# Where a two-layer diffusion block computes its second layer's modulation

## The chip, the cores and the metric

The kernel runs on one core of a Trainium2 chip. The metric is the device time of one execution in microseconds (us). A core has TensorE (PE; its weight loads run beside it as PEld), VectorE (DVE), ScalarE (ACT), GpSimd (POOL) and SyncE (SP, whose queue issues most transfers). Each engine takes its own instructions in order, and waits by semaphores for the others. Sixteen DMA engines move data between HBM and the on-chip memory.

## The reference

The block has two layers over 512 latent and 256 context tokens of width 1024. Layer 0 mixes by a bidirectional RWKV-7 recurrence and S5 channel groups, layer 1 by latent attention; each layer ends in a mixture of 16 experts. What the change touches:

```python
for layer in range(DEPTH):                       # DEPTH = 2
    m_l = split(silu(c) @ mod_w[layer] + mod_b[layer], 6)      # mod_w: 2 x 1024 x 6144 f32
    m_c = split(silu(c_ctx) @ mod_w[layer] + mod_b[layer], 6)
    a = modulate(rmsnorm(h, norm1_g[layer]), m[0], m[1])
    o = rwkv_s5_mixer(a, ...) if layer == 0 else mla_mixer(a, ...)
    h = h + m[2] * o
    f = modulate(rmsnorm(h, norm2_g[layer]), m[3], m[4])
    h = h + m[5] * moe_ffn(f, ...)
# in the recurrence: k_dir = k * (1 + (a - 1) * k_a); each token: S = S*w - sa*(a*kk) + v*k_dir; y = S @ r
# behind it, by token: (groupnorm(y) * ln_w + ln_b + bonus) * g
```

## The kernel before

The tokens are six tiles of 128. The program is written with a tile framework whose scheduler orders each engine's instructions by a model of their times; what is written early is not always placed early.

**Recurrence.** Steps s = 0 to 5 go over the tiles, forward and backward at once. For each step rwkv_stage_a (L544 and around it) makes decayed factors PQ and KB: VectorE writes the sums `wseg` (L518, L519) from the tile `ev`, scans them into E (L528), and the key factor passes through ACT (L544, scale and bias of `ta`), POOL (L546, times k) and DVE (L547, times E), using `ev` again as scratch. rwkv_stage_b then builds the matrices of a chunk: G from PE products (L572, L575); a 16 x 16 block of it goes through memory into A; X, a triangular inverse, is made on DVE by 15 pairs of L596 and L598; X is written out (L601) and comes back as D (L604). PE, ACT and DVE pass it on: pd0 (L612), Ta (L613), pd1 (L616), W (L617), pd2 (L620), G += (L624, eight DVE instructions), then pt20 to pt22 (L632, L637, L642) with ACT copies Tb between. rwkv_steps runs two half steps per tile: pU, VU, pZ (L697 to L704) and Z += (L706). The chain from G through X, D, G to Z is serial; S5 products (L1108, L1112), the outputs and the modulation are placed around it.

**Outputs.** rwkv_out(t) takes a tile's sums, normalizes them, gates them (gd, L746 to L750; pgate on PE) and stores them (18 larger DVE instructions for two tiles, L755 to L776). It is called at s = 3 for tiles 0 and 1, at s = 4 for 4 and 3, at s = 5 for 5 and 2. concat transposes them (ptcat, L1957) for the output projection.

**Modulation.** mod_part(l, q) makes a third of a layer's six vectors: 16 tiles `mw` of 512 KB from SP's queue (L162) through three buffers, eight matmul records each (L164, psmod), then bias and gain on DVE (L167, L169). The table MODN says behind which step the second layer's parts are written:

```python
MODN = {3: (0,), 4: (1,), 5: (2,)}
...
            if s in MODN:
                for q in MODN[s]:
                    self.mod_part(1, q, mp, ms, MODT)
```

Part 0 is used by the attention's input, parts 1 and 2 only behind the attention.

**Behind the experts** of layer 0 the kernel gathers each tile's expert outputs (POOL, cy), adds them to h (normed), transposes (ntt, L301), projects down (mla_down: pmi, L191 to L193, pmt), makes values (pv), and starts attention with pqp.

Of the kernel before, what the change touches and what calls it, by code (L numbers as in the profile page):

```python
# [16 lines left out]
F32 = mybir.dt.float32  # L17
# [3 lines left out]
AF = mybir.ActivationFunctionType  # L21
OP = mybir.AluOpType
# [13 lines left out]
ZT = ((0, 1, 2, 3, 4, 5), (1, 0, 5, 4, 3, 2))  # L36
# [8 lines left out]
MS14 = (4, 0, 5, 1, 6, 2, 7, 3, 12, 8, 9, 10, 11, 13)  # L45
MODT = "lo"
S5LATE = -800
MODN = {3: (0,), 4: (1,), 5: (2,)}


def dap(ap, offset, dims):
# [36 lines left out]
class Block:  # L88
# [35 lines left out]
    def cond(self, tp):  # L124
        nc, i = self.nc, self.i
        cr = tp.tile([16, 128], F32, name="cr")
        nc.sync.dma_start(cr[0:8, :], i["c"].rearrange("b (k p) -> (b k) p", p=128))
        nc.sync.dma_start(cr[8:16, :], i["c_ctx"].rearrange("(k p) -> k p", p=128))
        cs = tp.tile([16, 128], F32, name="csil")
        nc.scalar.activation(cs, cr, AF.Tanh, scale=0.5)  # L130
        nc.vector.tensor_scalar(cs, cs, 0.5, 0.5, op0=OP.mult, op1=OP.add)
        nc.vector.tensor_tensor(cs, cs, cr, OP.mult)
        pt = self.psum("tp", "pt_c", 2)
        nc.tensor.transpose(pt[:, :16], cs, self.ident[:16, :16])
        self.cst = self.c0.tile([128, 8, 32], F32, name="cst")
        nc.gpsimd.memset(self.cst, 0.0)
        nc.vector.tensor_copy(self.cst[:, :, 0:2], pt[:, :16].rearrange("p (v k) -> p k v", v=2))

    def mod_part(self, l, q, wpool, spool, tag="mod"):

        nc, i = self.nc, self.i
        if l not in self.mods:
# [13 lines left out]
            nc.vector.tensor_scalar(mb[r0:r0 + 64, :], mb[r0:r0 + 64, :], 1.0, None, op0=OP.add)  # L156
        ps = self.psum(tag, f"psmod{l}{q}", 1)
        for k in range(8):
            for h in range(2):
                wt = wpool.tile([128, 4, 256], F32, name=f"mw{l}{q}{k}{h}", tag="mw")  # L160
                w = i["mod_w"][l, k * 128:(k + 1) * 128, q * 2048:q * 2048 + 2048].rearrange("p (j c) -> p j c", j=4)
                last = nc.sync.dma_start(wt, w[:, :, 256 * h:256 * h + 256])  # L162
                for j in range(4):
                    nc.tensor.matmul(ps[32 * j:32 * j + 32, 256 * h:256 * h + 256], self.cst[:, k, :], wt[:, j],  # L164
                                     start=(k == 0 and h == 0), stop=(k == 7), skip_group_check=True)
        mo = mb
        nc.vector.tensor_tensor(mo, ps, mb, OP.add)  # L167
# [309 lines left out]
    def rwkv_stage_a(self, s, sp, wp, tag=("gr",), bufs=2):  # L477

        nc = self.nc
        st = {}  # L480
        for z in range(2):
# [6 lines left out]
            ta = wp.tile([128, 4, 128], F32, name=f"ta{z}{s}", tag="ta", bufs=2)  # L488
# [15 lines left out]
            ev = wp.tile([128, 4, 128], F32, name=f"ev{z}{s}", tag="ev", bufs=2)  # L504
# [16 lines left out]
            for k in range(2):  # L521
                E = wp.tile([128, 8, 65], F32, name=f"E{k}{z}{s}", tag=f"E{k}", bufs=1)
                f = E.rearrange("p a b -> p (a b)")
# [15 lines left out]
            r, k, kk = rk[:, 0:4], rk[:, 4:8], rk[:, 8:12]  # L539
            nc.vector.tensor_tensor(put(PQ[:, :, 64:192]), spl(kk), ei, OP.mult)  # L540
            nc.vector.tensor_tensor(ends(PQ), spl(r), e1, OP.mult)
            t1 = ev
            for m in range(4):
                nc.scalar.activation(t1[:, m, :], ta[:, m, :], AF.Identity, scale=self.hka[:, 0, m:m + 1],  # L544
                                     bias=self.hka[:, 1, m:m + 1])
            nc.gpsimd.tensor_tensor(t1, t1, k, OP.mult)  # L546
            nc.vector.tensor_tensor(ends(KB), spl(t1), e3, OP.mult)  # L547
            nc.scalar.activation(ta, ta, AF.Copy, scale=-0.5, bias=-0.5)
            nc.gpsimd.tensor_tensor(ta, ta, kk, OP.mult)
            nc.vector.tensor_tensor(put(KB[:, :, 64:192]), spl(ta), e3, OP.mult)  # L550
# [880 lines left out]
        nc.vector.tensor_tensor(hh, hh, ps[:, 256:], OP.mult)  # L1431
        return hh

    def row_psum(self, rows, name):

        out = [self.psum("cb", f"{name}{hf}", 2) for hf in range(2)]
        for j in range(8):
            self.nc.tensor.matmul(out[j // 4][:, j % 4 * 128:j % 4 * 128 + 128], self.ident[0:8, j:j + 1].to_broadcast([8, 128]),
                                  rows, start=True, stop=True, skip_group_check=True)
        return out  # L1440
# [174 lines left out]
    def mla_values(self, t):  # L1615

        nc = self.nc
        ts = slice(t * 128, t * 128 + 128)
        for hh in range(2):
            hs = slice(hh * 8, hh * 8 + 8)  # L1620
            ps = self.psum("ca", f"pv{t}{hh}", 2)
            self.mm3(ps, (self.kvT[0][:, ts], self.kvT[1][:, ts]), [x[:, hs, :].rearrange("p h c -> p (h c)") for x in self.kw],
                     True, True)
            dst, src = self.vv[:, t, hs], ps.rearrange("p (h c) -> p h c", h=8)
            if hh:
                nc.vector.tensor_copy(dst, src)
            else:
                nc.scalar.activation(dst, src, AF.Copy)

    def mla_down(self, aT, t, sp):  # L1630
# [8 lines left out]
        else:  # L1639
            nc.tensor.matmul(ps[:, 0:416], self.tri[0:1, 1], self.mwb, start=True, stop=False)  # L1640
            for k in range(8):
                self.mm3(ps[:, 0:416], (aT[0][:, k], aT[1][:, k]), (self.mwi[0][:, k], self.mwi[1][:, k]), False, k == 7)
        pt = self.psum("cb", f"pmt{t}", 2)
        if t >= 2:
            r = self.rstd_of(sp, ps[:, 0:256], f"mq{t}", 256)
            qn = sp.tile([128, 256], F32, name=f"qn{t}", tag="qn", bufs=2)
            nc.vector.scalar_tensor_tensor(qn, ps[:, 0:256], r, self.qnb, op0=OP.mult, op1=OP.mult)
            for k in range(2):
                nc.tensor.transpose(pt[:, k * 128:(k + 1) * 128], qn[:, k::2], self.ident)
        r = self.rstd_of(sp, ps[:, 256:384], f"mk{t}", 128)  # L1650
        kn = sp.tile([128, 128], F32, name=f"kn{t}", tag="kn", bufs=2)
        nc.vector.scalar_tensor_tensor(kn, ps[:, 256:384], r, self.kvb, op0=OP.mult, op1=OP.mult)
        nc.tensor.transpose(pt[:, 256:384], kn, self.ident)
        pe = sp.tile([128, 32], F32, name=f"kpe{t}", tag="kpe", bufs=2)
# [231 lines left out]
    def rwkv(self, es, s5d, rwd):  # L1886
# [25 lines left out]
        for s in range(6):  # L1912
# [11 lines left out]
            if s == 3:  # L1924
# [2 lines left out]
                self.rwkv_out_pre(op)  # L1927
                mp = self.pool("mwp1", 3, es=es)
                ms = self.pool("msp1", 1, es=es)
            if s == 3:  # L1930
                for t in (0, 1):
                    self.rwkv_out(t, op, rwd)
            elif s > 3:
                ends = {ZT[z][s]: self.rwkv_out(ZT[z][s], op, rwd if s < 5 else None, yy[z]) for z in range(2)}
            if s in MODN:
                for q in MODN[s]:
                    self.mod_part(1, q, mp, ms, MODT)
# [22 lines left out]
    def build(self):  # L1960
# [7 lines left out]
        with ExitStack() as es:  # L1968
# [10 lines left out]
            with ExitStack() as ec:  # L1979
# [5 lines left out]
        mes = ExitStack()  # L1985
        self.ffn(0, cat, hts, self.src_rows, i["hy_w_out"], ces,
                 lambda: self.mla_weights(self.pool("mlaw", 1, es=mes, side="right")))
        with ExitStack() as e0:
            kp = self.pool("mlk", 1, es=e0)
            self.rq = kp.tile([128, 2, 16, 96], F32, name="mqu")  # L1990
# [7 lines left out]
            with ExitStack() as e1:  # L1998
# [3 lines left out]
                sp = self.pool("mls", 1, es=e1, side="right")  # L2002
                g2c = [bp.tile([128, D], F32, name=f"g2c{v}") for v in range(2)]
                for v in (1, 0):
                    for hf, ps in enumerate(self.row_psum(self.g2r[:, v], f"g2c{v}")):
                        nc.scalar.activation(g2c[v][:, hf * 512:hf * 512 + 512], ps, AF.Copy)
                self.mla_split(wp)

                def normed(t):
                    h = hts[t]  # L2010
                    self.combine(self.fetch(0, t, xp, 2), h, g2c[int(t < 2)],
                                 (nc.vector, nc.vector if t < 2 else nc.gpsimd))
                    if t >= 2:
                        nc.sync.dma_start(self.hb[(t - 2) * 128:(t - 1) * 128], h)
                    r = self.rstd_of(xp, h, f"n1{t}")
                    return self.norm_tile(h, r, t, self.mc1, xp)

                nxt = normed(0)
# [148 lines left out]
```

## Time and profile before

| | us |
|---|---|
| median of three runs | 1959.4 (1953.17 to 1964.0) |
| the profiled execution, its own time | 1948.41 |
| its span, first to last instruction | 1946.6 |
| TensorE busy | 1563.9 (80%) |
| VectorE busy | 1218.9 (63%) |
| ScalarE busy | 774.2 (40%) |
| GpSimd busy | 701.3 (36%) |
| mean granted TensorE clock | 0.88 of full speed |

Busy shares are averages over stages. The stages lie in the span so: input projection to about 330 us, recurrence and S5 to 854, output projection and routing to 1050, experts to 1268, the down projections to 1378, attention to 1600, the second layer's experts and the final norm behind it. Times of a place are read from the span's start.

### The profile page before, as it was taken

How to read it: one execution, taken by the hardware profiler on the slowest of the kernel's cores; microseconds unless marked ns; L12 is line 12 of the kernel's file. 1: busy time of each engine (PE TensorE's matmuls, PEld its weight loads, DVE VectorE, ACT ScalarE, POOL GpSimd, SP SyncE). 2: the span in 40 equal slices, each digit the busy share in tenths (PEclk: the TensorE clock that was granted, in tenths of full speed). 3: DMA queues.
4: the chain of work that ended last, by engine and by line, in shares of the span. 5: the costliest groups of instructions: out<-in, count | busy, mean ns of one | idle time of the engine just before them, and what ended most of it. 6: DMA issues, size and time to landing. Idle time of an engine off the chain costs nothing. (4 is left out here: it accounts for less than half of the span.)

```text
span 1946.6 us, 32507 instructions
## 1 busy us (share of the span) xinstructions
PE 1563.9 (80%) x12531; PEld 1126.9 (58%) x12531; DVE 1218.9 (63%) x2385; ACT 774.2 (40%) x1434; POOL 701.3 (36%) x700
## 2 busy tenths in 40 slices
PE   5698898558687789649698999949699998789993
PEld 2376767447576655337575666638455556666662
DVE  4799933884866867243754654475678854575544
ACT  4222324334543523132413555433556543335542
POOL 0476802441423414102514233451143353324432
PEclk8688999678898869679899999969799998899997
DMA  8754587723233268743605999852000009349965
GB/s 257 213 174 157 164 275 218 218 60 109 62 88 103 72 223 258 241 170 128 246 33 188 389 354 367 328 175 65 1 1 1 1 0 367 110 168 370 377 230 184
DMA packets 222854, 347.65 MB, mean 179 GB/s; under 512 B 49538, under 2 KB 170296, under 8 KB 207784
## 3 DMA queue, kind: packets, MB, share of 16 engines
q1 hardware_dynamic: 206784, 294.71, 45.4%
q0 software_dynamic: 10080, 44.04, 6.3%
q10 hardware_dynamic: 5832, 6.78, 1.1%
q8 instruction: 100, 1.64, 0.3%
q14 instruction: 58, 0.48, 0.1%
HBM read 279.02 MB, written 66.46 MB: 177 GB/s over the span
## 5 line engine op out<-in xcount | busy, mean ns | idle before, releaser
L164 PE MATMUL psmod<-mw,cst 128*32 128x256 f32 x768 | 83.8, 491 | 43.5 <-DMA mw<-in_mod_w_dram 39.2
L191 PE MATMUL pwi<-aT,wih 128*128 128x256 f32 (+1 forms) x224 | 81.7, 367 | 14.4 <-DVE q L334 7.2
L192 PE MATMUL pwi<-aT,wih 128*128 128x256 f32 (+1 forms) x224 | 81.9, 367 | 0.0
L193 PE MATMUL pwi<-aT,wil 128*128 128x512 f32 (+1 forms) x224 | 81.2, 364 | 0.0
L1784 ACT ACTIVATE P<-st 128x512 f32<-128x512 f32 x96 | 56.9, 596 | 48.7 <-PE st L1782 44.7
L1797 POOL TENSOR_TENSOR sum<-sum,P 128x512 f32<-128x512 f32 x48 | 63.6, 1348 | 27.8 <-ACT P L1784 27.6
L1112 PE MATMUL s5y<-s5tq,s5H 128*96 128x128 f32 x256 | 50.6, 333 | 27.3 <-POOL s5H L1104 15.1
L1415 POOL DMA_INDIRECT xg<-fbuf,rk x36 | 37.8, 1051 | 92.9 <-PE ptx L231 52.3
L572 PE MATMUL pg<-PQ,KB 64*128 64x128 f32 x384 | 54.1, 318 | 18.7 <-ACT ta L501 10.4
L1098 POOL TENSOR_TENSOR s5t<-s5G,s5tq 128x384 f32<-128x384 f32 x16 | 18.0, 1123 | 141.5 <-DVE s5G L1095 121.3
L185 ACT ACTIVATE xT<-ptx 128x512 fp32r<-128x512 f32 x72 | 41.2, 596 | 66.1 <-PE ptx L231 65.0
L164 PEld LDWEIGHTS psmod<-mw,cst 128*32 128x32 f32 x768 | 20.3, 124 | 77.4 <-DMA mw<-in_mod_w_dram 55.7
L186 DVE TENSOR_TENSOR xT<-ptx,xT 128x512 fp32r<-128x512 f32 x72 | 48.2, 688 | 23.1 <-ACT xT L185 22.2
L572 PEld LDWEIGHTS pg<-PQ,KB 64*128 64x128 f32 x384 | 44.1, 211 | 31.2 <-ACT ta L501 10.7
L191 PEld LDWEIGHTS pwi<-aT,wih 128*128 128x128 f32 x224 | 46.2, 208 | 22.3 <-issue 11.4
L1112 PEld LDWEIGHTS s5y<-s5tq,s5H 128*96 128x96 f32 x256 | 37.8, 198 | 35.9 <-POOL s5H L1104 16.8
L1795 POOL TENSOR_TENSOR sum<-P,P 128x512 f32<-128x512 f32 x16 | 20.5, 1300 | 105.3 <-ACT P L1784 105.2
L231 PEld LDWEIGHTS ptx<-ident,xg 128*128 128x128 f32 x288 | 40.6, 192 | 26.6 <-issue 21.0
L1788 PE MATMUL po<-P,vv 128*64 128x512 f32 x192 | 54.3, 617 | 1.1 <-ACT P L1784 1.1
L685 PE MATMUL pU<-Z,PQ 128*64 128x128 f32 x192 | 30.3, 331 | 27.9 <-ACT Z L677 27.7
L231 PE MATMUL ptx<-ident,xg 128*128 128x128 f32 x288 | 42.9, 285 | 10.9 <-issue 7.0
L192 PEld LDWEIGHTS pwi<-aT,wih 128*128 128x128 f32 x224 | 46.1, 206 | 7.8 <-issue 3.1
(1569 smaller groups left out, 5161.0 us busy)
## 6 DMA issues: line engine op xcount, KB each, us to landing
mw<-in_mod_w_dram SPq DMA_DIRECT2D x96, 512.0 KB
yb<-yo SPq DMA_DIRECT2D x36, 512.0 KB
s5tq<-s5t SPq DMA_DIRECT2D x16, 960.0 KB
yb<-zrow SPq DMA_DIRECT2D x16, 512.0 KB
wi<-in_hy_w_in_dram SPq DMA_DIRECT2D x14, 512.0 KB
rk<-qbuf SPq DMA_DIRECT2D x12, 512.0 KB
fbuf<-f SPq DMA_DIRECT2D x10, 512.0 KB
s5t<-s5CP SPq DMA_DIRECT2D x4, 1152.0 KB
```

Source lines behind the costliest of these rows:

```text
L164: nc.tensor.matmul(ps[32 * j:32 * j + 32, 256 * h:256 * h + 256], self.cst[:, k, :], wt[:, j], start=(k == 0 and h == 0), stop=(k == 7), s ...
L185: nc.scalar.activation(hi, src, AF.Copy)
L186: nc.vector.tensor_tensor(lo, src, hi.bitcast(F32), OP.subtract)
L191: nc.tensor.matmul(out, lh, rh, start=start, stop=False, **kw)
L192: nc.tensor.matmul(out, lh, rl, start=False, stop=False, **kw)
L193: nc.tensor.matmul(out, ll, rh, start=False, stop=stop, **kw)
L231: nc.tensor.transpose(pt[:, k * 128:(k + 1) * 128], a[:, h * 4 + k::8], self.ident)
L572: nc.tensor.matmul(pg[hp][:, m], KB[rs, m, ps2], PQ[rs, m, ps2], start=True, stop=True, skip_group_check=True)
L1112: nc.tensor.matmul(out, H[:, g, d, k, h0:h0 + 96], CP[:, k, d, i0:i0 + 8, :].rearrange("p a b -> p (a b)"), start=False, stop=(d == 1 and ...
L1784: ex = nc.scalar.activation(P, st, AF.Exp, scale=SCALE)
L1788: mm = nc.tensor.matmul(po[64 * x:64 * x + 64], vv[:, kt, h0 + x, :], P, start=(kt == 0), stop=(kt == 5), skip_group_check=True)
L1797: nc.gpsimd.tensor_tensor(sums[x], sums[x], P, OP.add)
```

## The change

Three edits. (1) Parts 1 and 2 of the second layer's modulation are no longer made in the recurrence but behind the first layer's experts, in 32 tiles of 256 KB each instead of 16 of 512 KB, through four buffers of their own; for that the PSUM tags there are divided anew, and the small matrix cst is made again from a kept copy. (2) The outputs of tiles 0 and 1 are called at s = 4, behind those of tiles 4 and 3, instead of at s = 3. (3) The key factor is written by ACT straight into KB and multiplied there in place by POOL and DVE; `ev` is no longer its scratch. Besides, squares for the norms behind the experts go into tiles that exist.

```diff
-MODN = {3: (0,), 4: (1,), 5: (2,)}
+MODN = {3: (0,)}
...
-        nc.vector.tensor_copy(self.cst[:, :, 0:2], pt[:, :16].rearrange("p (v k) -> p k v", v=2))
-
-    def mod_part(self, l, q, wpool, spool, tag="mod"):
+        self.cs2 = self.cp.tile([128, 8, 2], F32, name="cst2")
+        nc.vector.tensor_copy(self.cs2, pt[:, :16].rearrange("p (v k) -> p k v", v=2))
+        nc.vector.tensor_copy(self.cst[:, :, 0:2], self.cs2)
+
+    def mod_part(self, l, q, wpool, spool, tag="mod", parts=2, bufs=None):
...
-            for h in range(2):
-                wt = wpool.tile([128, 4, 256], F32, name=f"mw{l}{q}{k}{h}", tag="mw")
+            for h in range(parts):
+                n = 512 // parts
+                wt = wpool.tile([128, 4, n], F32, name=f"mw{l}{q}{k}{h}", tag="mw", bufs=bufs)
                 w = i["mod_w"][l, k * 128:(k + 1) * 128, q * 2048:q * 2048 + 2048].rearrange("p (j c) -> p j c", j=4)
-                last = nc.sync.dma_start(wt, w[:, :, 256 * h:256 * h + 256])
+                last = nc.sync.dma_start(wt, w[:, :, n * h:n * h + n])
                 for j in range(4):
-                    nc.tensor.matmul(ps[32 * j:32 * j + 32, 256 * h:256 * h + 256], self.cst[:, k, :], wt[:, j],
+                    nc.tensor.matmul(ps[32 * j:32 * j + 32, n * h:n * h + n], self.cst[:, k, :], wt[:, j],
                                      start=(k == 0 and h == 0), stop=(k == 7), skip_group_check=True)
...
-            t1 = ev
             for m in range(4):
-                nc.scalar.activation(t1[:, m, :], ta[:, m, :], AF.Identity, scale=self.hka[:, 0, m:m + 1],
+                nc.scalar.activation(ends(KB)[:, m], spl(ta)[:, m], AF.Identity, scale=self.hka[:, 0, m:m + 1],
                                      bias=self.hka[:, 1, m:m + 1])
-            nc.gpsimd.tensor_tensor(t1, t1, k, OP.mult)
-            nc.vector.tensor_tensor(ends(KB), spl(t1), e3, OP.mult)
+            nc.gpsimd.tensor_tensor(ends(KB), ends(KB), spl(k), OP.mult)
+            nc.vector.tensor_tensor(ends(KB), ends(KB), e3, OP.mult)
...
-            ps = self.psum("ca", f"pv{t}{hh}", 2)
+            ps = self.psum("cb", f"pv{t}{hh}", 3)
...
-        pt = self.psum("cb", f"pmt{t}", 2)
+        pt = self.psum("cb", f"pmt{t}", 3)
...
-            r = self.rstd_of(sp, ps[:, 0:256], f"mq{t}", 256)
             qn = sp.tile([128, 256], F32, name=f"qn{t}", tag="qn", bufs=2)
+            r = self.rstd_of(sp, ps[:, 0:256], f"mq{t}", 256, sq=qn)
...
-            if s == 3:
+            if s > 3:
+                ends = {ZT[z][s]: self.rwkv_out(ZT[z][s], op, rwd if s < 5 else None, yy[z]) for z in range(2)}
+            if s == 4:
                 for t in (0, 1):
                     self.rwkv_out(t, op, rwd)
-            elif s > 3:
-                ends = {ZT[z][s]: self.rwkv_out(ZT[z][s], op, rwd if s < 5 else None, yy[z]) for z in range(2)}
...
+        mp = self.pool("mwp2", 1, es=mes, side="right")
+        self.cst = mp.tile([128, 8, 32], F32, name="cst1")
+        nc.gpsimd.memset(self.cst, 0.0)
+        nc.vector.tensor_copy(self.cst[:, :, 0:2], self.cs2)
+        self.ppes.close()
+        self.psum_pool(None, "ppm")
...
                 self.mla_split(wp)
+                for q in (1, 2):
+                    self.mod_part(1, q, mp, mp, "md", 4, 4)
 
                 def normed(t):
                     h = hts[t]
-                    self.combine(self.fetch(0, t, xp, 2), h, g2c[int(t < 2)],
+                    ys = self.fetch(0, t, xp, 2)
+                    self.combine(ys, h, g2c[int(t < 2)],
                                  (nc.vector, nc.vector if t < 2 else nc.gpsimd))
...
-                    r = self.rstd_of(xp, h, f"n1{t}")
+                    r = self.rstd_of(xp, h, f"n1{t}", sq=ys[1])
```

In the new file the recurrence's lines have moved by two or three (L624 is L626, L706 is L708, L164 is L167).

On PE, in the last tile's chain (s = 5) from pd2 to pt22, before the change (psmod is the modulation, ptcat the concat's transpose):

```order
L620 MATMUL pd_8532<-D_2729,W_2730 32x32 x64
L164 MATMUL psmod_9168<-mw_9193,cst 32x256 x4
L164 MATMUL psmod_9168<-mw_9199,cst 32x256 x4
L164 MATMUL psmod_9168<-mw_9205,cst 32x256 x4
L632 MATMUL pt_8606<-ident,G_8253 32x32 x16
L632 MATMUL pt_8606<-ident,G_8299 32x32 x16
L164 MATMUL psmod_9168<-mw_9211,cst 32x256 x4
L1957 MATMUL ptcat_9307<-ident,cy_9305 128x128 x4
L637 MATMUL pt_8641<-Tb_8605,G_8253 32x32 x16
```

and the same place after it:

```order
L622 MATMUL pd_8460<-D_2731,W_2732 32x32 x64
L1138 MATMUL s5zt_7820<-ident,zt_6819 128x96 x4
L752 MATMUL pgate_9029<-gup,gd_9025 128x512
L634 MATMUL pt_8534<-ident,G_8181 32x32 x16
L634 MATMUL pt_8534<-ident,G_8227 32x32 x16
L1144 MATMUL s5gl_7827<-s5zT_7813,s5glu 128x256
L639 MATMUL pt_8569<-Tb_8533,G_8181 32x32 x16
```

The psmod instructions are gone from the chain; S5's small products and a gate stand there, and ptcat stands behind the first half step.

On DVE, ahead of the eight instructions that make G (L624, now L626) in the same chain, before:

```order
L1137 COPY s5zT_7811<-s5zt_7818 128x96x4
L1144 SCALAR_TENSOR_TENSOR s5zT_7811<-s5sg_7824,s5zT_7811 128x256
L156 TENSOR_SCALAR mb_9159<-mb_9159 64x512
L1144 SCALAR_TENSOR_TENSOR s5zT_7811<-s5sg_7829,s5zT_7811 128x512
L624 TENSOR_TENSOR G_8253<-D_2729,pd_8532 32x8x32
```

and after (yo_8720 and yo_8757 are the outputs of tiles 0 and 1, gn1nt a scratch of their norm):

```order
L777 TENSOR_TENSOR yo_8720<-yo_8720,gw_8713 128x512
L226 SCALAR_TENSOR_TENSOR ri_8770<-gn1nt,ri_8770 128x8
L778 TENSOR_TENSOR yo_8720<-yo_8720,vo_8714 128x512
L776 TENSOR_TENSOR yo_8757<-yo_8757,ri_8770 128x512
L626 TENSOR_TENSOR G_8181<-D_2731,pd_8460 32x8x32
```

Nearly all of the outputs' instructions of tiles 0 and 1 now stand between X and G of the last tile; before, they stood in tile 4's chain. X itself now begins on DVE ahead of the last Z of tile 4, with six of its 30 instructions left behind that Z; before, all of them stood behind it.

On PE, at the end of the down projections, the new order has (pv are the values of the last tile, pqp the attention's first matmul):

```order
L196 MATMUL pv_13101<-kwv_11982,kvT_11936 128x512
L196 MATMUL pv_13106<-kwv_11982,kvT_11936 128x512
L167 MATMUL psmod_12221<-mw_12378,cst_11921 32x128 x4
L167 MATMUL psmod_12221<-mw_12384,cst_11921 32x128 x4
L167 MATMUL psmod_12221<-mw_12390,cst_11921 32x128 x4
L167 MATMUL psmod_12221<-mw_12396,cst_11921 32x128 x4
L167 MATMUL psmod_12221<-mw_12402,cst_11921 32x128 x4
L167 MATMUL psmod_12221<-mw_12408,cst_11921 32x128 x4
L194 MATMUL pqp_13189<-qT_11933,qwp_13181 128x512
```

Before, pqp stood right behind pv. Of the 64 new tiles' psmod groups 12 stand ahead of the first ntt, eight among ntt and pmi of the first tiles, 21 among the later pmi and pv, and 23 from the last tile's pmi on. Four loads of mw stand in SP's queue among the experts' first loads, the other 60 behind the experts' last store.

## Rows read from the trace of the kernel before

**Rows 1.** the page, parts 1 and 5 (idle time before a group, releaser)
```profile
PE 1563.9 (80%) x12531; PEld 1126.9 (58%) x12531; DVE 1218.9 (63%) x2385; ACT 774.2 (40%) x1434; POOL 701.3 (36%) x700
...
L164 PE MATMUL psmod<-mw,cst 128*32 128x256 f32 x768 | 83.8, 491 | 43.5 <-DMA mw<-in_mod_w_dram 39.2
```

**Rows 2.** busy time by stretch: us, busy (x instructions) of each engine, granted clock, DMA share, GB/s
```profile
700.00:750.00 50.00, 50.00 (x604) 32.02 (x602) 29.54 (x69) 18.20 (x37) 13.91 (x23) 0.81 0.81 248
750.00:800.00 50.00, 39.63 (x421) 21.30 (x420) 36.84 (x102) 13.07 (x26) 16.23 (x23) 0.80 0.69 219
800.00:854.00 54.00, 37.36 (x898) 24.24 (x898) 8.11 (x17) 12.64 (x28) 0.52 (x1) 0.77 0.60 190
...
1050.00:1268.00 218.00, 206.71 (x830) 142.02 (x828) 118.26 (x132) 116.89 (x170) 75.57 (x50) 1.00 0.93 345
1268.00:1301.00 33.00, 8.01 (x33) 3.14 (x32) 25.50 (x79) 13.25 (x25) 17.58 (x11) 0.66 0.54 172
1301.00:1325.00 24.00, 19.83 (x94) 19.36 (x95) 21.57 (x49) 5.51 (x16) 17.69 (x12) 0.78 0.61 199
1325.00:1378.00 53.00, 46.51 (x205) 38.99 (x204) 27.46 (x113) 19.46 (x63) 0.91 (x4) 0.92 0.05 16
```

**Rows 3.** instructions in time, ACT then DVE, tile 4's chain: start, us, instruction [idle before]
```profile
678.00 1.65 ACT L544 ACTIVATE ev<-ta,hka 128x128 f32<-128x128 f32 x4 [7.88 <-DVE wseg L519]
679.55 0.57 ACT L613 ACTIVATE Ta<-pd 128x512 f32<-128x512 f32 x1
...
694.10 0.23 DVE L748 TENSOR_SCALAR gd<-gd 128x128 f32<-128x128 f32 x1 [4.07 <-ACT gd L747]
694.30 3.05 DVE L624 TENSOR_TENSOR G<-D,pd 32x256 f32<-32x256 f32 x8
...
697.98 0.96 DVE L762 TENSOR_TENSOR yo<-yo,yo 128x512 f32<-128x512 f32 x1
...
728.31 0.69 DVE L776 TENSOR_TENSOR yo<-yo,vo 128x512 f32<-128x512 f32 x1
```

**Rows 4.** DVE in time, the marks of the last tile's chain
```profile
755.53 1.38 DVE L706 TENSOR_TENSOR Z<-pZ,Z 64x512 f32<-64x512 f32 x2
...
757.48 0.17 DVE L596 TENSOR_TENSOR xt<-X,A 128x15 f32<-128x15 f32 x1
...
781.19 0.18 DVE L598 TENSOR_TENSOR X<-X,xt 128x15 f32<-128x15 f32 x1
...
810.13 3.07 DVE L624 TENSOR_TENSOR G<-D,pd 32x256 f32<-32x256 f32 x8 [2.04 <-PE pd L620]
...
852.98 1.41 DVE L706 TENSOR_TENSOR Z<-pZ,Z 64x512 f32<-64x512 f32 x2 [8.98 <-PE pZ L704]
```

**Rows 5.** SP's queue in time, between X and D of the last tile
```profile
782.87 1.15 SPq L601 DMA_DIRECT2D xo<-X  x2
785.98 4.62 SPq L162 DMA_DIRECT2D mw<-in_mod_w_dram  x2
790.69 7.85 SPq L604 DMA_DIRECT2D D<-xo  x16
```

**Rows 6.** PE in time, from G on, last tile
```profile
816.80 1.08 PE L164 MATMUL psmod<-mw,cst 128*32 128x256 f32 x8 [6.15 <-DMA mw<-in_mod_w_dram]
818.27 1.08 PE L164 MATMUL psmod<-mw,cst 128*32 128x256 f32 x8 [0.39 <-DMA mw<-in_mod_w_dram]
819.28 1.92 PE L632 MATMUL pt<-ident,G 32*32 32x32 f32 x64
...
840.56 0.64 PE L164 MATMUL psmod<-mw,cst 128*32 128x256 f32 x8 [1.24 <-DMA mw<-in_mod_w_dram]
```

**Rows 7.** one line, L544: what its engine waited for, us in total, times
```profile
  DVE wseg L519: 39.0, 7
```

**Rows 8.** PE in time, behind the experts
```profile
1301.15 4.17 PE L301 MATMUL ntt<-ntd,h 128*128 128x128 f32 x16 [24.84 <-issue]
...
1377.66 0.76 PE L191 MATMUL pqp<-qT,qwp 128*128 128x512 f32 x1 [0.83 <-ACT ngm L1687]
```

More of the change, by code (lines that the diff above doesn't have):

```diff
@@ L1432, in expert_mm, with row_psum @@
         return hh
-    def row_psum(self, rows, name):
-        out = [self.psum("cb", f"{name}{hf}", 2) for hf in range(2)]
+    def row_psum(self, rows, name, tag="cb", bufs=2):
+        out = [self.psum(tag, f"{name}{hf}", bufs) for hf in range(2)]
         for j in range(8):
@@ L1649, in mla_down @@
                 nc.tensor.transpose(pt[:, k * 128:(k + 1) * 128], qn[:, k::2], self.ident)
-        r = self.rstd_of(sp, ps[:, 256:384], f"mk{t}", 128)
         kn = sp.tile([128, 128], F32, name=f"kn{t}", tag="kn", bufs=2)
+        r = self.rstd_of(sp, ps[:, 256:384], f"mk{t}", 128, sq=kn)
         nc.vector.scalar_tensor_tensor(kn, ps[:, 256:384], r, self.kvb, op0=OP.mult, op1=OP.mult)
@@ L2004, in build @@
                 for v in (1, 0):
-                    for hf, ps in enumerate(self.row_psum(self.g2r[:, v], f"g2c{v}")):
+                    for hf, ps in enumerate(self.row_psum(self.g2r[:, v], f"g2c{v}", "cb", 3)):
                         nc.scalar.activation(g2c[v][:, hf * 512:hf * 512 + 512], ps, AF.Copy)
                 self.mla_split(wp)
+                for q in (1, 2):
+                    self.mod_part(1, q, mp, mp, "md", 4, 4)
                 def normed(t):
                     h = hts[t]
-                    self.combine(self.fetch(0, t, xp, 2), h, g2c[int(t < 2)],
+                    ys = self.fetch(0, t, xp, 2)
+                    self.combine(ys, h, g2c[int(t < 2)],
                                  (nc.vector, nc.vector if t < 2 else nc.gpsimd))
```

## The prediction

> **What bounds the kernel now.** I read the page first, then a table of busy time by stretch, then the stretches the change touches instruction by instruction. [rows 1] say that TensorE is busy for 80% of the span, an average over stages with different limits, and that the 96 modulation tiles made it wait 39.2 us for their loads. In [rows 2] the reader is to see three kinds of stretch. In the recurrent part TensorE is full from 700 to 750, then busy for 39.63 us of 50 and 37.36 of 54: there no engine is the limit, but a chain that runs from engine to engine. The experts run at a DMA share of 0.93 and 345 GB/s: loads bound them. From 1268 to 1301 TensorE does 8 us of work, from 1325 to 1378 it is busy for 46.51 of 53 us while the DMA engines idle (0.05). So the change takes matmuls and loads out of a chain, and puts them where first nothing, and then TensorE, is the limit.
>
> The chain of the last tile (s=5): the state Z of tile 4 ends; the triangular inverse X is built on VectorE; X goes to memory and back as D through SP's queue; three TensorE/ScalarE stages end in G (L624); four more end in Z (L706). [rows 4] give its marks: Z at 755.5, X begins at 757.5 and ends at 781.4, G at 810.1, last Z at 853.0.
>
> **The change, part by part.**
>
> (a) Tile 4's chain (s=4). [rows 3]: G at 694.30 starts when VectorE is through with a gate instruction of tiles 0 and 1, for which it had waited 4.07 us; that leaves. ScalarE waited 7.88 us at L544 for VectorE, and the chain's next copy (L613) stood behind it; that wait goes too, but how long L613's own input had been there the rows don't tell. The 18 VectorE instructions of those outputs, 0.7 us each, the first at 697.98, the last at 728.31, leave this stretch, but TensorE is full there, so they alone free little. The bounds are 4 us (the gate wait alone) and 14 us (both waits, 12 us, and a little of VectorE's time). I take -8, the gate wait and half the other.
>
> (b) X of s=5. From Z to the end of X 25.8 us pass today, because X's 30 small instructions share VectorE with two tiles' outputs and stand behind Z. In the new order all but six stand ahead of Z. Behind Z (1.4 us) I count six larger output instructions (0.7 us), the six of X (0.2) and six scans, which I put at 0.3, an estimate between the two: 8.6 us, and some waiting. I take 13 instead of 26: -13 (bounds -8 and -18).
>
> (c) X to G: 28.8 us now. In [rows 5] SP issues X at 782.87 and D only at 790.69, since two modulation loads waited for a buffer in front of it for 4.62 us; without them D goes about 7 us sooner. Against it, the outputs of tiles 0 and 1 now stand on VectorE between X and G: the same 18 instructions, 12 us, plus tile 4's and 3's last ones and the S5 part, which I estimate at as much again. The path alone would take 22 us (28.8 less 7), VectorE's queue 24, and with its waits for ScalarE up to 36. I take 0, the bounds are -7 and +7.
>
> (d) G to the last Z: 39.8 us. [rows 6]: G is ready at 813.2, but its transposes (L632) start at 819.28, because TensorE takes its instructions in order and two modulation tiles stood ahead, one of them 6.15 us late. Behind it further tiles stand between the stages, the last at 840.56. Eleven tiles of 0.64 to 1.08 us leave, and waits like the 1.24 us before the last; part of both lay under ScalarE's copies. Bounds -6 (the one wait) and -14; I take -12, as TensorE sits in the path at each of the stages. The two transposes that move behind the half step are 2 us either way.
>
> (e) Key factors in place. ScalarE's waits at L544 were 39 us in seven places [rows 7]. Most had cover: the product that ends the step needs VectorE's scan anyway, which comes after the same sums. Bounds 0 and -10; I take -4. The three instructions keep their sizes.
>
> (f) Loads of four tiles (1.05 MB) among the experts', at 345 GB/s [rows 2]: +3 us.
>
> (g) The stage behind the experts. TensorE now has 24.84 us idle before the first ntt [rows 8]; the new order puts 12 of 64 small tiles there. A 512 KB tile takes TensorE 0.64 us at the upper clock level and 1.08 at the lower [rows 6]; one of half the columns lies between 0.32 and 0.64 (or 0.5 and 1.08): 12 of them fit into the idle time and cost nothing. Eight more come up to 1325, 4 to 8 us, against 4.2 us idle there: +2. The next 21 lie between matmuls of a full TensorE: 21 x 0.45 = +9. The last 23 stand close together before the attention's first matmul (pqp, 1377.66 in [rows 8]), by the order among what were the last 15 us or so before it (an estimate), with four buffers. Their pace is that of loads. In [rows 6] eleven 512 KB tiles came between 816.80 and 840.56, with three buffers: 2.38 us each, 220 GB/s. At the same bytes per second a 256 KB tile comes every 1.2 us; at the experts' 345 GB/s every 0.76; and if a turn of the buffers keeps its 7.1 us, every 1.8. Nineteen tiles that are not yet loaded: 23 us against 15, +8 (bounds 0 and +19). Behind the last one VectorE adds the bias and gain (two of 0.7 us) ahead of the splits that pqp needs: +3. Together +22, with bounds +7 and +40. The scratch tiles that normed and mla_down now share only tie a gather to the square two tiles before: 0, as the twelve tiles ahead of the first ntt keep TensorE busy meanwhile; without that cover a late gather would move the ntt by a few us.
>
> The Trainium skill, "DMA: Bandwidth & Descriptors", in "Anatomy of one DMA — SWDGE (gpsimd) path", fits one transfer by 2.0 us plus its bytes over 436 GB/s, and in "Rules for kernel authors" asks for 1 MiB and more a transfer. By the fit, for another issuing path, 512 KB with three in flight would come every 1.07 us, and the trace shows 2.38, so it doesn't hold here; for 256 KB with four in flight it gives 0.65, and (g) would lose its +8 (an estimate by that page).
>
> **Sum.** -8 -13 +0 -12 -4 +3 +22 = -12 us. The profiled execution took 1948.41 us (span 1946.6), so 1936.4, a ratio of 0.9938; on the median of the runs shown, 1959.4, that is 1947. The runs lie between 1953 and 1964; about 0.5%, 10 us, is what a measurement of this kernel can tell from no change.
>
> **Rivals.**
>
> Given back. VectorE's queue, not the path, decides G, so that (c) is +7, and (g) is +26, its last tiles at 1.4 us: -12 +7 +4 = -1: 1958. For it: VectorE is already busy for 36.84 of 50 us there. Against it: in (c) the outputs' loads come early, so the instructions can run while X is away.
>
> Loads hidden. If the tiles behind the experts come at 0.76 us, and TensorE takes them at 0.32, (g) is +7 and the sum -27: 1932. For it: a DMA share of 0.05 from 1325 on. Against it: the 2.38 us of [rows 6], and the gathers that use the same engines until 1320.
>
> Slower: TensorE at its lower level behind the experts. The stretch 1325 to 1378 ran at a mean granted clock of 0.92, while those in which TensorE waits for modulation loads ran at 0.77 to 0.81 [rows 2], and the tile behind the 6.15 us wait took 1.08 and not 0.64 us. If the stage becomes such a stretch, the 46.51 us of its own work grow: at 0.78 by 8 us, at the lower level throughout by 39. The sum changes sign at 12 us, that is below a clock of about 0.73; with +30, which is 0.56, the time is 1977. For it: 64 waits where there were none. Against it: between the tiles lies work that needs no load.
>
> The Trainium skill, "TensorE: Matmul & The Clock Gate", in "HAM oscillation — how this bites in real kernels", says that matmuls which wait for each next load run cold again and again; the clocks of 0.77 to 0.81 agree with it in direction. It is the rule that speaks against this change.
>
> The chain unmoved. If (a) to (d) only shift which engine waits, the gain is the removed load and queue waits alone, 6 + 5 us, and the loss of +25 stays: +14, 1973. For it: TensorE is full from 700 to 750, and the first part stays there. Against it: the waits at L748, in SP's queue and at L632 have the moved work by name.
>
> **Chances.** Forecast (1947, own range 1937 to 1950) 0.36; given back 0.28; loads hidden 0.15; lower level 0.11; chain unmoved 0.10. Faster by over 0.5% is the first and the third, less a little of the first: 0.49. Slower by over 0.5% is the last two, less a little: 0.19. Within: 0.32. The range takes in loads hidden below, and the unmoved chain and the beginning of the lower level above: 1925 to 1974.
>
> **What would show it.** In the new trace: no psmod row between L614 and L711 of the last chain; Z to X 13 us, X to G about 29, G to the last Z about 28. Behind the experts, pqp about 22 us later than the end of the experts puts it now, with psmod rows that wait for mw in front of it, and a clock of 0.8 or more. I am wrong if G waits for the outputs of tiles 0 and 1 for more than 10 us, if the stage behind the experts loses over 40, or if tile 4's chain is as long as before because of the first modulation part, which stays there.

## The result, and the profile after

The changed kernel takes 1975.67 us (median of six runs, 1972.06 to 1978.12), the kernel before 1954.26 us in the six runs beside it (1948.65 to 1964.0): a ratio of 1.0098, with a 95% interval of 1.0073 to 1.0123. It is slower by 1.0%, and the forecast was 0.6% faster. The profiled execution spans 1970.4 us, at a mean granted clock of 0.864, where 1946.6 was before.

The page, part 5, the row of the modulation:

```profile
L167 PE MATMUL psmod<-mw,cst 128*32 128x256 f32 (+1 forms) x1024 | 84.3, 411 | 47.9 <-DMA mw<-in_mod_w_dram 42.7
```

The psmod rows wait no less for loads than before (43.5 in [rows 1]); these waits have only moved. ACT's key-factor line (L546, L544 before), who waited for it, us in total, times:

```profile
  POOL KB L548: 60.2, 6
```

ACT's 39.0 us at the key factor [rows 7] are all gone: that line has no wait left. But GpSimd, which waited 30.7 us for the factor before, now waits 60.2, of which 49.0 in one wait.

Busy time by stretch (columns as in [rows 2]; the last stretch ends where attention now begins):

```profile
750.00:800.00 50.00, 39.10 (x533) 27.22 (x533) 38.56 (x113) 16.57 (x38) 21.57 (x35) 0.89 0.44 131
800.00:854.00 54.00, 35.95 (x806) 28.28 (x806) 30.29 (x63) 22.58 (x42) 10.19 (x9) 0.69 0.36 121
1268.00:1301.00 33.00, 22.09 (x178) 11.34 (x177) 21.53 (x70) 11.37 (x22) 13.08 (x10) 0.69 0.79 246
1301.00:1325.00 24.00, 21.38 (x145) 17.70 (x146) 14.43 (x30) 4.99 (x14) 16.13 (x12) 0.86 0.86 284
1325.00:1400.00 75.00, 63.96 (x528) 45.57 (x527) 34.29 (x126) 19.62 (x61) 7.25 (x10) 0.87 0.54 160
```

In the last chain VectorE's work grew from 8.11 to 30.29 us and the transfers fell: the outputs came, the modulation went. Behind the experts TensorE fills its hole (8.01 to 22.09 us), then needs 75 us where it had 53, at a clock of 0.87.

VectorE in time, step 3's last Z, then the marks of the last chain, in the order of [rows 4]:

```profile
679.97 1.39 DVE L708 TENSOR_TENSOR Z<-pZ,Z 64x512 f32<-64x512 f32 x2 [7.52 <-PE pZ L706]
...
765.14 0.27 DVE L598 TENSOR_TENSOR xt<-X,A 128x15 f32<-128x15 f32 x1 [4.16 <-DMA A<-nt]
...
778.63 1.38 DVE L708 TENSOR_TENSOR Z<-pZ,Z 64x512 f32<-64x512 f32 x2
...
787.60 0.53 DVE L600 TENSOR_TENSOR X<-X,xt 128x15 f32<-128x15 f32 x1
...
818.54 0.68 DVE L776 TENSOR_TENSOR yo<-yo,ri 128x512 f32<-128x512 f32 x1
819.14 3.07 DVE L626 TENSOR_TENSOR G<-D,pd 32x256 f32<-32x256 f32 x8
...
848.25 1.41 DVE L708 TENSOR_TENSOR Z<-pZ,Z 64x512 f32<-64x512 f32 x2 [8.75 <-PE pZ L706]
```

X begins 13.5 us ahead of tile 4's Z and ends 9.5 us behind it (25.8 before). From G to the last Z 29.1 us pass (42.9 before). Yet that Z is only 4.7 us earlier (853.0 before): tile 4's Z, at 778.6, is 23.1 us late (755.5 before), and 19.8 of them are there at step 3's Z already (660.16 before, row below). The loss lies ahead of the chain that the forecast worked out in detail.

SP's queue between X and D: [rows 5] had 7.8 us from one to the other, and two modulation loads between.

```profile
788.15 1.11 SPq L603 DMA_DIRECT2D xo<-X  x2
789.35 0.54 SPq L762 DMA_DIRECT2D yo<-yd  x1
790.13 7.43 SPq L606 DMA_DIRECT2D D<-xo  x16
```

Now it is 2.0 us. The pd2 matmuls that G needs ended at 813.7, and G began at 819.1, behind the yo row shown above. Its transposes follow at once, where they came 6.1 us behind the end of G before ([rows 4], [rows 6]):

```profile
822.35 1.92 PE L634 MATMUL pt<-ident,G 32*32 32x32 f32 x64 [7.30 <-DVE G L626]
```

TensorE behind the experts; the first attention matmul stood at 1377.66 in [rows 8]:

```profile
1376.29 0.57 PE L167 MATMUL psmod<-mw,cst 128*32 128x128 f32 x8 [2.10 <-DMA mw<-in_mod_w_dram]
1377.07 2.23 PE L167 MATMUL psmod<-mw,cst 128*32 128x128 f32 x24 [0.21 <-DMA mw<-in_mod_w_dram]
...
1395.80 0.43 PE L167 MATMUL psmod<-mw,cst 128*32 128x128 f32 x8 [0.36 <-DMA mw<-in_mod_w_dram]
1400.68 0.80 PE L194 MATMUL pqp<-qT,qwp 128*128 128x512 f32 x1 [4.45 <-ACT qwp L188]
```

Eight matmuls are one tile: nineteen come between the first and the third row, 18 steps in 19.5 us, 1.08 us each. Then pqp waits 4.45 us for its split operand, behind the bias, the gain and a transfer of the result.

### The profile page after: what moved, and what is told of

It is laid out like the page before. It is cut to its first block, busy times and chain, and to the rows that moved or that the text cites. A ratio compares the mean times of both kernels' runs of the same rounds, so it can differ in the third digit from the quotient of the medians.

```text
span 1970.4 us, 33078 instructions
## 1 busy us (share of the span) xinstructions
PE 1594.7 (81%) x12787; PEld 1154.8 (59%) x12787; DVE 1212.2 (62%) x2387; ACT 771.4 (39%) x1432; POOL 699.2 (35%) x701
## 5 line engine op out<-in xcount | busy, mean ns | idle before, releaser
L167 PE MATMUL psmod<-mw,cst 128*32 128x256 f32 (+1 forms) x1024 | 84.3, 411 | 47.9 <-DMA mw<-in_mod_w_dram 42.7
L194 PE MATMUL pwi<-aT,wih 128*128 128x256 f32 (+1 forms) x224 | 82.4, 370 | 11.8 <-DVE s5w L993 8.7
L167 PEld LDWEIGHTS psmod<-mw,cst 128*32 128x32 f32 x1024 | 25.9, 122 | 88.8 <-DMA mw<-in_mod_w_dram 62.1
L1114 PE MATMUL s5y<-s5tq,s5H 128*96 128x128 f32 x256 | 55.2, 356 | 23.1 <-POOL s5H L1104 18.2
L189 DVE TENSOR_TENSOR xT<-ptx,xT 128x512 fp32r<-128x512 f32 x72 | 48.1, 687 | 25.8 <-ACT xT L188 24.5
L1797 POOL TENSOR_TENSOR sum<-P,P 128x512 f32<-128x512 f32 x16 | 20.5, 1301 | 102.6 <-ACT P L1786 102.5
L196 PEld LDWEIGHTS pwi<-aT,wil 128*128 128x128 f32 x224 | 46.7, 209 | 7.0 <-issue 2.2
```

Of the source, the lines that this page charges most:

```text
L167: nc.tensor.matmul(ps[32 * j:32 * j + 32, n * h:n * h + n], self.cst[:, k, :], wt[:, j], start=(k == 0 and h == 0), stop=(k == 7), skip_gr ...
L189: nc.vector.tensor_tensor(lo, src, hi.bitcast(F32), OP.subtract)
L194: nc.tensor.matmul(out, lh, rh, start=start, stop=False, **kw)
L196: nc.tensor.matmul(out, ll, rh, start=False, stop=stop, **kw)
L1114: nc.tensor.matmul(out, H[:, g, d, k, h0:h0 + 96], CP[:, k, d, i0:i0 + 8, :].rearrange("p a b -> p (a b)"), start=False, stop=(d == 1 and ...
```

## The experiments

Each was timed in five rounds beside the kernel before. "Step 3's Z" is the last Z += of the fourth tile pair, "last Z" that of the chain's end.

**Each edit by itself.** First the key factors, in the kernel before:

```
+ ACT writes ends(KB)[:, m];  POOL: ends(KB) *= spl(k);  DVE: ends(KB) *= e3     (no other edit)
```

> The kernel before with the key factors in place and nothing else. Theory A (this edit alone lengthened steps 0 to 3 of the recurrence by 20 us): 15 to 25 us slower than before, the second Z of step 3 near 680 us instead of 660. Rival B (the modulation's new place made the scheduler order the early steps anew): within 4 us of before, step 3's second Z at 660.

1975.06 us, 1.011 [1.0081, 1.0138]: this edit alone costs 21 us. The mark, in the kernel before, then here:

```profile
660.16 1.38 DVE L706 TENSOR_TENSOR Z<-pZ,Z 64x512 f32<-64x512 f32 x2
```

```profile
683.97 1.39 DVE L705 TENSOR_TENSOR Z<-pZ,Z 64x512 f32<-64x512 f32 x2 [2.85 <-ACT ta L501]
```

Step 3's Z is 23.8 us late, and no modulation or output has moved; the last Z, at 883.1, is 30 us late. Then the change without this edit:

```
- ACT writes ends(KB) ...          (edits 1 and 2 as in the change)
+ t1 = ev; ACT writes t1; POOL: t1 *= k; DVE: ends(KB) = t1 * e3
```

> The changed kernel with the key factors made in the scratch tile as before. Theory A: some 20 us faster than the changed kernel, within 6 us of the kernel before; step 3's second Z back at 660, the stage behind the experts as long as in the changed kernel (134 us from the last expert matmul to pqp). Rival B: as slow as the changed kernel.

1946.38 us, 0.9949 [0.9925, 0.9974]: 7.6 us faster than before, and 29 us faster than the changed kernel, where 20 were expected. Step 3's Z stands at 663.3, the last Z 38 us sooner than before, and attention begins at 1374.3:

```profile
815.02 1.41 DVE L709 TENSOR_TENSOR Z<-pZ,Z 64x512 f32<-64x512 f32 x2 [3.48 <-PE pZ L707]
```

The forecast's terms without (e) make -8, but the agreement is of two errors: up to the last Z it is -38 here, where (a) to (d) make -33, and from the last Z to attention it is +35, not +25. Then edit 2 alone, and edit 1 alone (with the norms' squares):

```
  if s > 3: ... rwkv_out of 4, 3 (s = 4), of 5, 2 (s = 5)
+ if s == 4: rwkv_out of 0, 1      (only this, in the kernel before)
```

> The kernel before with the outputs of tiles 0 and 1 called at s = 4 and nothing else. Theory A says nothing of it. If the outputs in the last chain cost what the changed trace shows (X to G 31 us although the queue in front of D was free), this alone is 0 to 8 us slower, since the modulation still stands in that chain; if they free tile 4's chain as I forecast, it is up to 8 us faster.

```
+ MODN = {3: (0,)}, parts 1 and 2 behind the experts      (only this)
```

> The kernel before with modulation parts 1 and 2 moved behind the experts (and the squares' scratch that goes with it), outputs and key factors as before. From the changed trace: last chain 28 us shorter or a little more, the stage behind the experts 25 us longer, loads among the experts 2 us: between 8 us faster and no change. If the outputs' move was needed for the gain, it is 5 us or more slower.

The outputs' move alone: 1935.36, 0.9888 [0.9863, 0.9914]. The modulation's alone: 1970.6, 1.0079 [1.0055, 1.0102]. The first gains 19 us, more than either case expected; the second is 17 us slower, the case in which the outputs' move is needed for the gain. With the first, X ends at 757.8, before tile 4's Z (761.3), and the last Z comes at 823.6. There the end of the loads takes over; TensorE, and the stretch ahead of it by engine, in that kernel:

```profile
858.40 1.22 PE L191 MATMUL po<-wo000hi,cat 128*128 128x512 f32 x2 [9.92 <-ACT wo000hi L185]
```

```profile
825.00:858.40 33.40, 14.87 (x109) 6.70 (x105) 19.76 (x42) 10.40 (x17) 0.78 (x6) 0.61 0.96 335
```

The output projection waits 9.92 us for its weights, while the DMA engines are at 0.96: 29 us were gained in the chain, 20 are left at po. With the modulation's move alone X still ends 27.4 us behind tile 4's Z (25.8 before), X to G falls from 28.8 to 18.7, G to Z from 42.9 to 33. So (b) is the outputs' doing, and the waits in SP's queue and on TensorE are the modulation's.

**The stage behind the experts.** Both have the old key factors. One leaves out seven eighths of the moved sums (128 of the 1024 input rows, eight tiles instead of 64), the other puts only part 2 behind the experts:

```
- for k in range(8):  (64 tiles in parts 1 and 2)
+ for k in range(1):  (8 tiles)
```

> The changed kernel with old key factors, and behind the experts only an eighth of parts 1 and 2 (the first 128 of 1024 input rows: 8 tiles instead of 64); the rest of these sums is left out. Prices the stage: my forecast put 22 us on it and 3 on the loads among the experts, the changed trace shows 25 from the last expert matmul to pqp. So 20 to 30 us faster than the run with all 64 tiles (1946); if the stage is long for another reason (the new PSUM tags, the gathers), under 10.

```
- MODN = {3: (0,)};          for q in (1, 2): ... behind the experts
+ MODN = {3: (0,), 4: (1,)}; for q in (2,): ...
```

> Outputs of tiles 0 and 1 at s = 4, old key factors, modulation parts 0 and 1 in the recurrence, only part 2 behind the experts. If behind the experts each tile costs what it did in the changed trace (25 us for 64), this part costs 12 to 15 us there and saves the 10 us that the output weights waited for the end of the modulation loads in the run with the outputs moved alone, and some 5 in the chain: within 6 us of that run (1935). If the cost there is mostly fixed: 1945 or more.

Eight tiles: 1915.08, 0.9804 [0.9786, 0.9821]. Thirty-two: 1928.12, 0.9885 [0.9866, 0.9904]. The last Z of these and of the kernel with 64 lies between 814.5 and 816.0, and attention begins at 1344.5, 1352.1 and 1374.3. So the first 24 tiles more cost 7.6 us, the next 32 cost 22.2. With 32 tiles, 12 stand ahead of the first ntt and the others end at 1324.5, 28 us ahead of the attention; with 64, the first 32 end at about 1326 as well, and the last only at 1369.7, 5 us ahead of it. The 56 tiles together cost 29.8 us up to the attention, where 20 to 30 were expected. The kernel with 32 has the lowest median of those that do all the work, and beats both kernels; its ratio can't be told from that of the outputs' move alone. An earlier placing of the loads, with the outputs' move alone, was tried against the wait for wo:

```
- MODN = {3: (0,), 4: (1,), 5: (2,)}
+ MODN = {3: (0, 1), 4: (2,)}
```

> Outputs of tiles 0 and 1 at s = 4, old key factors, all three modulation parts in the recurrence, but part 1 already at s = 3 and part 2 at s = 4. In the run with the outputs alone (1935) the last loads of part 2 made the output weights wait 10 us. If that wait is all that is to be had: 1925 to 1930. If the earlier chain, where TensorE is full, pays for it: 1935 to 1945.

1934.6, 0.9892 [0.9853, 0.9931], no more than without it: po comes at 862.5, since the last Z is now at 839.6.

**Why the key factors cost time.** Two kernels take the reasons apart. In one ACT's write into KB must wait as it did for `ev`, in the other the old three instructions use a scratch tile of their own, and nothing is in place:

```
+ held = ACT copies one column into ev;  the writes into KB are issued after it
```

> The kernel before with the key factors in place, but ScalarE held as before: it first writes one element per row of ev, which has to wait until VectorE has read ev, and the four key instructions are queued behind that. Theory A1 (the edit costs its 20 us because, without the wait, the scheduler orders S5's products and the next tile's factors differently around the chain): within 5 us of the kernel before. Theory A2 (writing and multiplying in KB itself is slower, or holds a buffer): 15 to 25 us slower.

```
- t1 = ev
+ t1 = a tile of its own
```

> The kernel before with the key factors in a scratch tile of their own instead of ev: nothing is done in place, but ScalarE need not wait for VectorE. Theory A1: 8 to 25 us slower than before, though nothing is in place, if the order again changes much. Theory A2: within 5 us of before, or faster.

The scratch of its own costs the same: 1968.87, 1.0107 [1.0071, 1.0144], step 3's Z at 684.2. So the arithmetic in place is not needed for the cost. Held, 1967.58, 1.0088 [1.006, 1.0115]: steps 0 to 2 are as before again (601.8 against 599.6), but step 3's Z is 11 us late and X of the last tile ends 45 us behind tile 4's Z (25.8 before). Within 5 us of the kernel before was expected of it, and it is 15 us slower, the edge of what the second theory (A2) had: the wait, given back, gives back neither the order nor the time, and a missing wait is not needed for a cost either. That the instructions in place cost it is spoken against by the runs with another order below, where they cost 5 us. What all these kernels share is a new order.

What the order does is to be seen in step 0, where 10.4 of the 23.8 us arise (its last Z is at 472.4 before, at 482.9 with the factors in place); the other steps were not taken apart. TensorE, first in the kernel before:

```profile
450.36 1.29 PE L1112 MATMUL s5y<-s5tq,s5H 128*96 128x128 f32 x4 [1.14 <-POOL s5H L1102]
452.36 1.17 PE L1112 MATMUL s5y<-s5tq,s5H 128*96 128x128 f32 x4 [0.71 <-POOL s5H L1104]
...
458.24 1.20 PE L704 MATMUL pZ<-VU,KT 128*64 128x64 f32 x32 [0.28 <-ACT VU L699]
```

and with the key factors in place alone:

```profile
451.32 0.74 PE L1111 MATMUL s5y<-s5tq,s5H 128*96 128x128 f32 x2 [5.03 <-POOL s5H L1101]
...
452.99 1.92 PE L641 MATMUL pt<-G,Tb 32*32 32x32 f32 x64
...
464.79 1.00 PE L1111 MATMUL s5y<-s5tq,s5H 128*96 128x128 f32 x4 [2.83 <-POOL s5H L1101]
466.79 1.17 PE L1111 MATMUL s5y<-s5tq,s5H 128*96 128x128 f32 x4 [0.99 <-POOL s5H L1103]
...
469.39 2.03 PE L703 MATMUL pZ<-VU,KT 128*64 128x64 f32 x32
```

The S5 matmuls, which nobody in the chain needs, now wait longer for GpSimd ahead of the chain's pt and pZ (5.03 us at pt, and 5.02 in the changed kernel). Why GpSimd is late, VectorE's and its rows in the kernel before:

```profile
424.56 1.59 DVE L1095 TENSOR_TENSOR_SCAN s5G<-s5a,s5G,s5t 128x63 f32<-128x63 f32 x2
...
426.23 1.78 POOL L1098 TENSOR_TENSOR s5t<-s5G,s5tq 128x384 f32<-128x384 f32 x1 [0.47 <-DVE s5G L1095]
```

and in place:

```profile
423.61 0.17 DVE L595 TENSOR_TENSOR xt<-X,A 128x15 f32<-128x15 f32 x1 [7.35 <-DMA A<-nt]
...
446.01 0.58 DVE L1094 TENSOR_TENSOR_SCAN s5G<-s5a,s5G,s5t 128x63 f32<-128x63 f32 x2
...
446.67 1.78 POOL L1097 TENSOR_TENSOR s5t<-s5G,s5tq 128x384 f32<-128x384 f32 x1 [2.46 <-DVE s5G L1094]
```

GpSimd now does the free factors ahead of S5's product (from 422.34 on; before, from 429.80 on, behind it). But they are not what that product waits for: GpSimd is idle for 8.55, 0.74 and 2.46 us behind them, the last for VectorE's S5 scan. That scan stands behind X and G on VectorE, and X begins 11.8 us later than before (411.84), after a wait for A; before, the scan stood ahead of G (436.90). So S5's product is 20 us late. From G to the first half step's Z, step 0 takes 33.6 us instead of 23.1, in the changed kernel 33.6 as well.

If it is the order, another order must give another price. S5LATE, the priority that places S5 (-800), was set to -400, in the kernel with the factors in place, in the kernel before, and in the changed kernel:

```
- S5LATE = -800
+ S5LATE = -400
```

> The kernel before with the key factors in place, and S5's priority in the scheduler put back by 400 places instead of 800: the same instructions as in the run with the key factors alone (1975, 21 us slower than before), in another order; on GpSimd the order is closer to that of the kernel before. Theory A1 (the order around the chain costs the 20 us, not the edit's instructions): the time moves by 8 us or more from 1975, most likely down. Theory A2 (the instructions cost it): 1970 to 1980.

> The kernel before with S5's priority put back by 400 instead of 800, nothing else: how far does an order alone move the time. Theory A1: by several us in either direction, 5 to 25. Theory A2: within 4 us of the kernel before.

> The changed kernel whole, with S5's priority put back by 400 instead of 800. If the 20 us of the key factors' edit are the order's and the three edits add up: the sum of this order with the key factors in place (0.2% faster than before) and of the two other edits (0.5% faster): 0.3 to 1.0% faster than the kernel before. If the order that helps goes with the old outputs alone: as slow as the changed kernel, 1% slower than before.

In place: 1952.06, 0.9979 [0.9951, 1.0007]; 23 us less (1.3% by the ratios), by the same instructions in another order. The kernel before: 1947.31, 0.995 [0.9923, 0.9977]. So the edit costs 21 us in one order and 5 us in the other, where the two intervals overlap. The changed kernel: 1956.43, 1.0023 [1.0005, 1.0042]; by the ratios it gets back 15 of its 19 us, but does not come out ahead of before as I had expected. In these three step 3's Z is still late (674 to 683, against 660.2): the time comes back in steps 4 and 5. So the runs with -400 show that the edit's price hangs on the order, and do not show that the waits of step 0 are that price. A late Z of step 3 by itself is no loss; in the kernel before with -400, which is 10 us faster, it comes at the changed kernel's time (679.97):

```profile
679.92 1.38 DVE L706 TENSOR_TENSOR Z<-pZ,Z 64x512 f32<-64x512 f32 x2
```

## Why the prediction was wrong

The step that failed is (e). It took the key factors as three instructions of unchanged size whose waits would go, and asked only how much of 39 us lay under other work: between 0 and -10. It measured +21 by itself, and +29 within the change, where the kernel without it takes 1946.38 us; in the trace it is +19.8 up to step 3's Z (680.0 instead of 660.2). The bounds had only one sign, because a wait that goes was taken as a wait gained. But with it gone the scheduler ordered steps 0 to 3 anew, on all engines. That this price hangs on the order is shown: a scratch tile without in-place writes costs the same, and the edit costs 21 us under one priority number and 5 under another. Which link of the order costs it stays open: how much are the waits shown, how much TensorE's lower clock in these steps (below), and why the held form, which has steps 0 to 2 as before, loses 15 us in steps 3 to 5.

(a) fell with it in this kernel: from step 3's Z to tile 4's it was 95.4 us and is 98.7, +3 instead of -8. ScalarE's wait and the gate's ahead of G are gone. But with the key factors in place alone (without ScalarE's wait) it is 98.3, with the outputs' move alone (without the gate's) 101.4, and in the changed kernel with the old factors 94.8: none comes near -8, and these two waits were not what set this stretch. The first modulation part stands in it still, from 719.8 to 763.2; whether it is the reason, which the forecast named as a sign of being wrong, was not tried.

(b) was right and too small: -16.3 (forecast -13, bounds -8 and -18). The two edits by themselves show that it is the outputs' move. Without the key factors' edit it is -30.0, as X then ends 4.1 us ahead of tile 4's Z; so that edit cost nearly half of this gain too. (c) +2.3, within +7 and -7. The two opposite things that it named are there, 5.8 us gained in SP's queue and G held 5.5 us by the outputs of tiles 0 and 1; two that it did not name are 1.5 us gained ahead of the queue, and 4.1 us lost from D's first issue to the end of pd2 (19.4 before, 23.6 now), where S5's matmuls that wait for GpSimd stand between the halves of pd0. (d) -13.7 (forecast -12): no psmod row is left in the chain, and G's transposes start 0.1 us behind the end of G, not 6.1. (f) +2.1 (forecast +3), from the last Z to the first expert result: 1.8 us shorter to po, 3.9 longer from there.

(g) was +25.4 from the last expert matmul to pqp (forecast +22). The last tiles came every 1.08 us, not 1.2. So the estimate from equal bytes per second was nearest. The fit of the Trainium skill ("DMA: Bandwidth & Descriptors", "Anatomy of one DMA — SWDGE (gpsimd) path") gives 0.65 us, an estimate by that page for another issuing path, and was too fast again for loads from SP's queue. With the experts' loads the stage's price was put at 25 us; leaving out 56 of the 64 tiles saves 28 (by the ratios) to 31.

Of the rivals, the lower clock did not come: 0.86 and 0.87 from 1301 on, where the sum would have turned at 0.73. Of the Trainium skill's rule on waits for each next load ("TensorE: Matmul & The Clock Gate", "HAM oscillation — how this bites in real kernels") the trace shows little: 0.87 instead of 0.92 in the last stretch, but 0.86 instead of 0.78 in the one before it. Loads hidden fell by (g). Given back is seen in part: VectorE's queue does decide G, for 5.5 us, and (g) is near its +26, but (c) is +2.3 and not +7, and the last tiles come at 1.08 us and not 1.4. Chain unmoved is not seen, as (b) and (d) are there. That the time nearly hit its 1973 is luck.

Added up: +19.8 +3.3 -16.3 +2.3 -13.7 = -4.6 at the last Z, 1.7 us shorter from there to po, then the experts' loads and the stage behind them: pqp is 23.0 us later, and the span 23.8.

## What to carry to other kernels

Under a scheduler that orders by modelled times, a removed dependency is a new order, not a saved wait: compare the two orders of every engine around the serial chain, ask what now stands ahead of the chain and what that waits for, and price the edit with bounds of both signs. Bring each edit of a bundle alone: here the outputs' move (-1.1%) was hidden by two others that cost 0.8 and 1.1% alone. When work is moved into a hole, move no more than ends well ahead of the next stage: with the outputs moved and the old factors, all of the loads behind the experts gave -0.5%, half of them -1.2%, and none of them -1.1%, which can't be told from the half.

## What was not expected of the hardware

VectorE's small instructions stretch when GpSimd multiplies. With the key factors in place alone, VectorE, and then GpSimd, at the same time:

```profile
425.18 0.21 DVE L597 TENSOR_TENSOR X<-X,xt 128x48 f32<-128x48 f32 x1
425.42 1.30 DVE L595 TENSOR_TENSOR xt<-X,A 128x55 f32<-128x55 f32 x1
426.76 1.19 DVE L597 TENSOR_TENSOR X<-X,xt 128x55 f32<-128x55 f32 x1
427.98 0.22 DVE L595 TENSOR_TENSOR xt<-X,A 128x60 f32<-128x60 f32 x1
```

```profile
425.38 1.27 POOL L548 TENSOR_TENSOR ta<-ta,rk 128x512 f32<-128x512 f32 x1 [1.77 <-ACT ta L547]
426.61 1.27 POOL L508 TENSOR_TENSOR ev<-ev,vv 128x512 f32<-128x512 f32 x1
```

An instruction of X that takes 0.22 us takes as long as the GpSimd instruction that it starts beside. The Trainium skill, "SBUF — State Buffer", "Who interferes with whom", has it that a VectorE instruction with two inputs in SBUF contends with a GpSimd instruction that reads SBUF, and that the port pair they share is an exclusive lock. The trace agrees: 1.19 to 1.33 us against 0.22. X of five tiles took 37.5 us of VectorE before, 50.0 with the factors in place, 47.0 in the changed kernel. The stretching does not set the time by itself: with the factors in place and S5LATE at -400 it is 52.3, in a kernel that is 23 us faster.

TensorE's granted clock is lower in step 0, and it was so before S5's waits came. The same two stretches of the kernel before, then with the factors in place:

```profile
380.00:437.00 57.00, 36.56 (x647) 30.74 (x645) 47.10 (x128) 17.17 (x42) 23.83 (x29) 0.77 0.27 68
437.00:484.00 47.00, 39.03 (x997) 33.02 (x999) 22.64 (x47) 20.82 (x47) 9.89 (x16) 0.87 0.39 113
```

```profile
380.00:437.00 57.00, 45.61 (x607) 40.14 (x606) 37.71 (x106) 15.58 (x40) 16.71 (x24) 0.56 0.25 65
437.00:484.00 47.00, 32.81 (x577) 27.66 (x580) 32.38 (x60) 16.18 (x35) 16.61 (x20) 0.69 0.32 94
```

From 437 it is 0.69 instead of 0.87, with TensorE busy for 32.81 us instead of 39.03, and pZ above takes 2.03 instead of 1.20 us. But from 380 to 437, ahead of the waits shown, it is 0.56 instead of 0.77 already, with TensorE busy for 45.61 us and not 36.56, on fewer matmuls. So the new order and a lower clock come together; that S5's waits lowered it is not shown.
